# Window attention of a two-layer encoder: queries and keys projected with features on partitions, the rotary partner crossed by DMA, a third PSUM bank for scores

## The chip, the cores and the metric

The kernel runs on one core of a Trainium2 chip. A core has a matmul engine (TensorE, PE in the profile, with its weight load PEld), a vector engine (DVE), a scalar engine (ACT), a general engine (GpSimd, POOL), a queue engine (SyncE, SP) that issues transfers, and 16 DMA engines. Matmul results land in PSUM, which has 8 banks of 128 x 512 floats. The metric is device time in microseconds (us) of one execution.

## The reference

The program is an encoder of two layers over 1024 tokens of width 1024. Layer 0 mixes tokens by windowed attention and by cross-attention into 256 memory tokens, layer 1 by a gated recurrence; each ends in a convolutional feed-forward. The change touches the windowed attention alone: 16 query heads of 64 features, 4 key/value heads, rotary positions on queries and keys, each token looking 128 tokens to either side, and one sink per head.

```python
def rope(x, pos):
    ...
    x1, x2 = xf[..., :half], xf[..., half:]
    return jnp.concatenate([x1 * cos - x2 * sin, x2 * cos + x1 * sin], axis=-1).astype(x.dtype)

def mixer_window_attn(u, mem_kv, w_in, sink, w_out, pos):
    q, k, v, xq = jnp.split(u @ w_in, [ATT_Q_W, ATT_Q_W + ATT_KV_W, ATT_Q_W + 2 * ATT_KV_W], axis=-1)
    q = rope(q.reshape(bsz, t, ATT_HEADS, ATT_HEAD_DIM), pos)
    k = rope(k.reshape(bsz, t, ATT_KV_HEADS, ATT_HEAD_DIM), pos)
    ...
    o = window_gqa_sink(q, k, v, sink).reshape(bsz, t, ATT_Q_W)
    return jnp.concatenate([o, memory_cross_attn(xq, mem_kv)], axis=-1) @ w_out
```

## The kernel before

Float32 precision is kept by splitting each operand into a high and a low part and adding three matmuls (`mm3`, L79 to L82). The input of layer 0 stands transposed in `uh` and `ul`, features on partitions and tokens along the row. Its norm factor per token, `rs0`, is not in there: it is multiplied into the rotary tables (for queries and keys) and into v afterwards (`rooted`, L1375).

`window()` works through four groups, one per key/value head with its four query heads. `proj(g)` loads four weight units of 128x768 (`wunit`: load on SP, high part on ACT, low part on DVE or, by `QKV_POOL`, on POOL). For each of 8 tiles of 128 tokens, `token(t)` makes 24 matmuls with the tile of `uh` held still and 384 weight columns moving (256 for queries, 64 keys, 64 values), so a result has tokens on partitions. DVE multiplies it by the cosines (L285) and, with the two halves of each head swapped by an access pattern, by the sines (L286); POOL adds the two (L287, L288); ACT and DVE take v out (L290, L298). `turn(b, rqs)` then transposes four tiles at a time on TensorE into the bank `ptq` (L310), since scores need features on partitions, and ACT and DVE split the result out of PSUM: keys by `split`, queries into tiles that hold the high part on one half of the partitions and the low part on the other (L318 to L321).

`attend` makes the scores of one block of 128 queries and one head against up to 384 keys in a bank `ps` (L362, L363); DVE adds the mask, takes the maxima and moves them to `sm` (L365), ACT takes the exponentials (L372), ACT and DVE divide (L381, L383), TensorE transposes the probabilities into `pt` (L388), ACT and DVE split them into `ph` and `pl` (L85, L86), and TensorE multiplies them with v into `po` (L391, L392). Cross-attention units stand between. PSUM is dealt out as two banks `pj` for projections, one `ptq`, two `ps`, two `pt` and one `po`: all eight.

The code is written as attend(g), then proj(g+1); a tile scheduler with a timeline model of its own mixes the two when the program is built, and fixes each engine's order of instructions. On the chip each engine runs its list in order and waits at semaphores. On POOL's queue hang transfers for the feed-forward (`second_sums`, L143), one step of them behind each rotary addition (`sum_steps[0].send(done)`).

Of the kernel before, what the change touches and what calls it, by code (L numbers as in the profile page):

```python
# [31 lines left out]
QKV_POOL = (0, 2, 2, 2)  # L32
# [14 lines left out]
def build(tc, A, out):  # L47
# [36 lines left out]
    def split(h, l, src):  # L84
        act.copy(h, src)  # L85
        dve.tensor_tensor(l, src, h.bitcast(F32), op=ALU.subtract)  # L86
# [155 lines left out]
    def window():  # L242
# [10 lines left out]
        c4 = lambda ap: ap.rearrange("p (h a c) -> p h a c", a=2, c=32)  # L253

        tags = {"pj": ("pj", 2, psq), "ps": ("ps", 2, psp), "pt": ("pt", 2, psp), "po": [lambda: psp.tile([P, 512], F32, tag="po", bufs=1, name="po")] * 2, "sm": 3}
        xhead = [None]
        def pair(kind, i):
# [3 lines left out]
        units = [(h, b) for h in range(4) for b in range(2)]  # L261

        def proj(g):
            us = [wunit(A["wqkv"][g, u], 768, eng=pool if u < QKV_POOL[g] else None) for u in range(4)]
# [5 lines left out]
            def token(t):  # L270
                ps = psq.tile([P, 384], F32, tag="pj", bufs=2, name="pj")
                for k in range(KT):
                    wh, wl = us[k // 2]
                    c = slice((k % 2) * 384, (k % 2 + 1) * 384)
                    m = slice(t * P, (t + 1) * P)
                    mm3(ps, uh[:, k, m], ul[:, k, m], wh[:, c], wl[:, c], k == 0, k == KT - 1)
                if g == 0:
                    with tc.issue_after(roped[0].ins) if t else nullcontext():
                        rooted(t, cos[:, t], sin[:, t].rearrange("p a b -> p (a b)"))
                t1 = ea.tile([P, 320], F32, tag="t1", bufs=1, name="t1")  # L280
                t2 = ea.tile([P, 320], F32, tag="t2", bufs=1, name="t2")
                rq = ea.tile([P, 384], F32, tag="rq", bufs=5, name="rq")
                cb = bc(cos[:, t, :].unsqueeze(1).unsqueeze(1), [P, 5, 2, 32])
                sb = bc(sin[:, t, :, :].unsqueeze(1), [P, 5, 2, 32])
                dve.tensor_tensor(c4(t1), c4(ps[:, :320]), cb, op=ALU.mult)  # L285
                roped[0] = dve.tensor_tensor(c4(t2), c4(ps[:, :320])[:, :, ::-1, :], sb, op=ALU.mult)  # L286
                pool.tensor_tensor(rq[:, :320], t1, t2, op=ALU.add)  # L287
                done = pool.tensor_tensor(rq[:, 320:], t1[:, 256:], t2[:, 256:], op=ALU.add)  # L288
                sum_steps[0].send(done)
                cast = act.activation(v[:, t, :64], ps[:, 320:], AF.Copy, scale=rs0[:, t:t + 1])  # L290
                if g == 0 and t + 5 < NT:
                    tag = ("kh", "kl", "v")[t]
                    row = ap_.tile([P, NT, P] if tag == "v" else [P, T], F32R, tag=tag, bufs=1, name="row").bitcast(F32)
                    row = row.rearrange("p a b -> p (a b)") if tag == "v" else row
                    nc.sync.dma_start(row, A["x"][(t + 5) * P:(t + 6) * P, :])
                    with tc.issue_after(cast.ins):
                        act.activation(row, row, AF.Square, accum_out=xss[:, t + 5:t + 6])
                dve.scalar_tensor_tensor(v[:, t, 64:], ps[:, 320:], rs0[:, t:t + 1], v[:, t, :64].bitcast(F32),  # L298
                                         op0=ALU.mult, op1=ALU.subtract)
                return rq  # L300

            def turn(b, rqs):
                hs = slice(b * 512, (b + 1) * 512)
                for w in range(3) if (g, b) not in ((0, 0), (3, 1)) else (2, 0, 1):
                    if g or b or w == 2:
                        tp = psq.tile([P, 4, P], F32, tag="ptq", bufs=1, name="ptq")
                    else:
                        tp = psp.tile([P, 4, P], F32, tag="pt", bufs=2, name="ptq")
                    for tt in range(4):
                        pe.transpose(tp[:, tt, :], rqs[tt][:, w * P:(w + 1) * P], ident)  # L310
                    tp = tp.rearrange("p a b -> p (a b)")
                    if w == 2:
                        split(kh[:, hs], kl[:, hs], tp)
                    else:
                        lo, hi = slice(0, 64), slice(64, 128)
                        q0, q1 = [ap_.tile([P, 512], F32R, tag="qs", bufs=8, name="qs") for _ in range(2)]
                        qs[2 * w][b], qs[2 * w + 1][b] = q0, q1
                        act.copy(q0[lo], tp[lo])  # L318
                        dve.tensor_tensor(q0[hi], tp[lo], q0[lo].bitcast(F32), op=ALU.subtract)
                        act.copy(q1[hi], tp[hi])  # L320
                        dve.tensor_tensor(q1[lo], tp[hi], q1[hi].bitcast(F32), op=ALU.subtract)  # L321

            kept = (qs, kh, kl, v)
            if g == 0:
                rqs = [token(t) for t in range(5)]
                turn(0, rqs[:4])
                attend(0, kept, range(3))
                turn(1, rqs[4:] + [token(t) for t in range(5, NT)])
            else:
                for b in range(2):  # L330
                    turn(b, [token(t) for t in range(4 * b, 4 * b + 4)])
            return kept

        pairs, roped = {}, {}
# [9 lines left out]
        def attend(g, qkv, blocks=range(NT)):  # L344
            qs, kh, kl, v = qkv
            for b in range(2):
                for nn in range(4):
# [11 lines left out]
                    for j in range(4):  # L359
                        s = psp.tile([P, 384], F32, tag="ps", bufs=2, name="ps")  # L360
# [66 lines left out]
        wo0.begin(psq, ("pj", "pj", "ptq"), [y0[:, t, :] for t in range(NT)], {6: marks[3, 2], 7: marks[3, 2]})  # L427
# [944 lines left out]
    cos = tables.tile([P, NT, 32], F32, name="cos")  # L1372
    sin = tables.tile([P, NT, 2, 32], F32, name="sin")

    def rooted(t, *turns):  # L1375
        c = slice(t, t + 1)
        dve.tensor_scalar(xss[:, c], xss[:, c], 1.0 / D, EPS, op0=ALU.mult, op1=ALU.add)
        pool.tensor_tensor(rs0[:, c], xss[:, c], nhalf[:, c], op=ALU.pow)
        for x in turns:
            dve.tensor_scalar_mul(x, x, rs0[:, c])  # L1380
# [110 lines left out]
def prepare(i):  # L1491
# [23 lines left out]
    for g in range(4):  # L1515
        w = np.concatenate([aw[:, 256 * g:256 * g + 256], aw[:, 1024 + 64 * g:1024 + 64 * g + 64],
                            aw[:, 1280 + 64 * g:1280 + 64 * g + 64]], axis=1)
        qkv.append(w.reshape(4, 2, P, 384).transpose(0, 2, 1, 3).reshape(4, P, 768))
# [32 lines left out]
    a["cos"] = c(co.reshape(NT, P, 32).transpose(1, 0, 2))  # L1551
    a["sin"] = c(np.stack([-si, si], 1).reshape(NT, P, 2, 32).transpose(1, 0, 2, 3))
# [20 lines left out]
```

## Time and profile before

| | |
|---|---|
| time, median of 3 runs | 2656.88 us (2653.15 to 2657.52) |
| profiled execution, its own time | 2650.18 us |
| its span | 2648.4 us |
| TensorE busy | 98% of the span |
| the stage that the change touches | from about 55 us to about 430 us |

In a group's row of the profile the columns are line, engine, operation, output and input names, shape, count, busy time, mean ns of one, and then the idle time of the engine just before such instructions with what ended it. Matmuls are pipelined, so that a matmul's duration is longer than the time by which it moves the next one.

### The profile page before, as it was taken

To read this page: it belongs to the slowest core of one execution; us is meant where nothing else is said; L and a number is where in the kernel's file an instruction comes from. 1 tells how busy PE (TensorE), PEld (TensorE's weight loads), DVE (VectorE), ACT (ScalarE), POOL (GpSimd) and SP (SyncE) were. 2 spreads that over 40 slices of the span, in tenths; PEclk is the share of its full clock that TensorE was granted. 3 is DMA by queue.
4 is the path that set the end of the run, shared out by engine and by line. 5 is a ranking of instruction groups with operands and counts; after the bars stand their busy time and mean duration, and the time that the engine had idled before them with its cause. 6 is when DMAs were issued, how large, how long until landed. Compare 5 with 4: busy or idle time off the path is not lost. (4 is left out here: it accounts for less than half of the span.)

```text
span 2648.4 us, 38975 instructions
## 1 busy us (share of the span) xinstructions
PE 2595.5 (98%) x14372; PEld 2177.9 (82%) x14372; DVE 1768.2 (67%) x2948; ACT 1395.1 (53%) x2534; POOL 473.0 (18%) x520
## 2 busy tenths in 40 slices
PE   8999999999999999999999999999999999999998
PEld 7888887788888888887888888888887788888887
DVE  6788886578565655477668685876657665656447
ACT  6467676545444445455465564656434444444443
POOL 0321010211111100031224241322211111110013
PEclk9999999999999999999999999999999999999999
DMA  9782222367777756674235351113337778785666
GB/s 355 249 174 57 74 86 85 102 192 196 199 198 199 206 153 219 215 267 158 84 104 152 87 131 51 55 33 114 121 108 194 197 195 204 202 203 169 202 209 235
DMA packets 195727, 425.92 MB, mean 161 GB/s; under 512 B 20048, under 2 KB 56272, under 8 KB 189904
## 3 DMA queue, kind: packets, MB, share of 16 engines
q1 hardware_dynamic: 161552, 324.06, 37.9%
q0 software_dynamic: 24544, 90.19, 16.4%
q10 hardware_dynamic: 9440, 9.19, 1.0%
q8 instruction: 113, 1.85, 0.3%
q14 instruction: 78, 0.64, 0.1%
HBM read 330.04 MB, written 116.39 MB: 169 GB/s over the span
## 5 line engine op out<-in xcount | busy, mean ns | idle before, releaser
L86 DVE TENSOR_TENSOR wl<-st,wh 128x1024 fp32r<-128x1024 f32 (+1 forms) x238 | 262.4, 1109 | 316.6 <-ACT wh L85 286.1
L85 ACT CAST wh<-st 128x1024 fp32r<-128x1024 f32 (+1 forms) x238 | 222.2, 936 | 287.7 <-PE X L574 189.3
L80 PE MATMUL pj<-uh,wh 128*128 128x512 f32 x512 | 203.9, 399 | 2.8 <-DVE q L1129 1.3
L574 PE MATMUL X<-wh,wl 128*128 128x512 f32 x528 | 205.2, 390 | 0.0
L574 PE MATMUL X<-wl,wh 128*128 128x512 f32 x528 | 205.1, 390 | 0.0
L81 PE MATMUL pj<-ul,wh 128*128 128x512 f32 x512 | 202.6, 396 | 0.0
L82 PE MATMUL pj<-uh,wl 128*128 128x512 f32 x512 | 202.3, 395 | 0.0
L574 PE MATMUL X<-wh 128*128 128x512 f32 x528 | 198.9, 390 | 0.6 <-DVE c L1003 0.6
L80 PE MATMUL pj<-wh,uh 128*128 128x384 f32 (+1 forms) x512 | 189.1, 371 | 3.4 <-DVE xl L86 1.3
L82 PE MATMUL pj<-wh,ul 128*128 128x384 f32 (+1 forms) x512 | 187.2, 366 | 0.0
L81 PE MATMUL pj<-wl,uh 128*128 128x384 f32 (+1 forms) x512 | 187.1, 365 | 0.0
L574 PE MATMUL V<-uh,wh 128*128 128x512 f32 x336 | 130.9, 390 | 0.0
L574 PE MATMUL V<-ul,wh 128*128 128x512 f32 x336 | 130.9, 390 | 0.0
L574 PE MATMUL V<-uh,wl 128*128 128x512 f32 x336 | 130.9, 390 | 0.0
L76 DVE TENSOR_TENSOR wl<-st,wh 128x1024 fp32r<-128x1024 f32 (+1 forms) x91 | 112.1, 1236 | 24.7 <-ACT wh L75 22.7
L75 ACT CAST wh<-st 128x1024 fp32r<-128x1024 f32 (+1 forms) x97 | 97.7, 1014 | 39.5 <-PE pj L81 16.4
L574 PEld LDWEIGHTS X<-wh 128*128 128x128 f32 x528 | 99.2, 188 | 21.4 <-issue 1.0
L574 PEld LDWEIGHTS X<-wl,wh 128*128 128x128 f32 x528 | 99.2, 188 | 20.5
L574 PEld LDWEIGHTS X<-wh,wl 128*128 128x128 f32 x528 | 99.2, 188 | 20.5
L80 PEld LDWEIGHTS pj<-uh,wh 128*128 128x128 f32 x512 | 96.3, 188 | 22.0 <-DVE q L1129 1.8
L962 POOL TENSOR_TENSOR c<-c,g 128x512 f32<-128x512 f32 x24 | 43.8, 1843 | 389.3 <-PE X L574 319.4
L1225 POOL TENSOR_TENSOR E<-EP,q 128x256 f32<-128x256 f32 x64 | 61.4, 959 | 288.9 <-DVE EP L1218 272.7
(411 smaller groups left out, 7219.1 us busy)
## 6 DMA issues: line engine op xcount, KB each, us to landing
st<-hid SPq DMA_DIRECT2D x154, 256.0 KB, 3.2
st<-in_ffw_dram SPq DMA_DIRECT2D x108, 256.0 KB, 3.5
w2s<-in_ffw_dram POOLq DMA_DIRECT2D x24, 1024.0 KB, 8.4
st<-in_ffw_dram SPq DMA_DIRECT2D x46, 512.0 KB, 4.4
hid<-tt SPq DMA_DIRECT2D x88, 256.0 KB, 4.7
st<-w2s SPq DMA_DIRECT2D x88, 256.0 KB, 3.4
sx<-in_ffw_dram SPq DMA_DIRECT2D x84, 256.0 KB, 3.9
sy<-in_ffw_dram SPq DMA_DIRECT2D x42, 512.0 KB, 6.5
```

The costliest lines, as they stand in the source:

```text
L75: act.copy(h[:, :n], raw)
L76: (eng or dve).tensor_tensor(l[:, :n], raw, h[:, :n].bitcast(F32), op=ALU.subtract)
L80: pe.matmul(o, ah, bh, start=first, stop=False)
L81: pe.matmul(o, ah, bl, start=False, stop=False)
L82: return pe.matmul(o, al, bh, start=False, stop=last)
L85: act.copy(h, src)
L86: dve.tensor_tensor(l, src, h.bitcast(F32), op=ALU.subtract)
L574: last = pe.matmul(o, x, y, start=new, stop=e, skip_group_check=not first)
L962: pool.tensor_tensor(y[q][:, t, :], y[q][:, t, :], g3[:, c], op=ALU.mult)
L1225: pool.tensor_tensor(gl, pl_, ql, op=ALU.mult)
```

## The change

Features now stand on partitions from the start. A group's weights come as three units of 128x1024: one with 64 value and 64 key columns, two with 128 query columns (two heads) each. `project(u, b)` holds 128 weight columns still and moves 512 tokens, so one unit and one half of the tokens is 24 matmuls of 512 columns, and ACT copies the result to memory (`raw`, L304). The partner half of each head for the rotation is on other partitions, so DMAs on SP cross it over (`swapped`, L309). DVE multiplies the product by the cosines, POOL the crossed copy by the sines (L312), and POOL adds (L313); ACT and DVE split the sum, from memory in place of PSUM (L349 to L352, L85, L86). The 64 key rows are laid down twice, on both halves of the partitions, by DMA (L322). Values are transposed back to tokens on TensorE (L326). The tables become 128x1024 each and are scaled by a matmul of ones with the diagonal of the token factors (`scaled_tables`). The freed `ptq` bank becomes `ps2`, a third bank for scores, used for every third score tile.

```diff
-QKV_POOL = (0, 2, 2, 2)
+QKV_POOL = (0, 1, 1, 1)
...
+        def score():
+            scored[0] += 1
+            if scored[0] % 3:
+                return psp.tile([P, 384], F32, tag="ps", bufs=2, name="ps")
+            return psq.tile([P, 384], F32, tag="ps2", bufs=1, name="ps")
...
+        def temp(tag):
+            return ea.tile([P, 512], F32, tag=tag, bufs=2, name=tag)
+
+        def scaled_tables(b):
+            hs = slice(b * 512, (b + 1) * 512)
+            rooted(slice(4 * b, 4 * b + 4))
+            dg = temp("t1").rearrange("p (a b) -> p a b", a=4)
+            bank = psp.tile([P, 4, P], F32, tag="pt", bufs=2, name="pbc")
+            for t in range(4):
+                dve.tensor_scalar_mul(dg[:, t], ident, rs0[:, 4 * b + t:4 * b + t + 1])
+                pe.matmul(bank[:, t, :], ones, dg[:, t], start=True, stop=True)
+            bank = bank.rearrange("p a b -> p (a b)")
+            for x in (cos, sin):
+                dve.tensor_tensor(x[:, hs], x[:, hs], bank, op=ALU.mult)
...
+            def project(u, b):
+                hs = slice(b * 512, (b + 1) * 512)
+                wh, wl = us[u]
+                ps = psq.tile([P, 512], F32, tag="pj", bufs=2, name="pj")
                 for k in range(KT):
...
+                    c = slice(k * P, (k + 1) * P)
+                    mm3(ps, wh[:, c], wl[:, c], uh[:, k, hs], ul[:, k, hs], k == 0, k == KT - 1)
+                raw = temp("qa")
+                act.copy(raw, ps)
+                return ps, raw, hs
+
+            def swapped(o, lo, raw, at):
+                for a, z in ((0, 32), (32, 0)):
+                    nc.sync.dma_start(o[lo + a:lo + a + 32], raw[at + z:at + z + 32])
+
+            def rope(a, x, hs):
+                pool.tensor_tensor(x, x, sin[:, hs], op=ALU.mult)
+                done = pool.tensor_tensor(a, a, x, op=ALU.add)
+                for _ in range(2 if sent[0] % 3 == 0 else 1):
+                    sum_steps[0].send(done)
+                sent[0] += 1
+
+            def keys(b):
+                ps, raw, hs = project(0, b)
+                x, a = temp("qb"), temp("t1")
+                for lo in (0, 64):
+                    nc.sync.dma_start(a[lo:lo + 64], raw[64:])
+                    swapped(x, lo, raw, 64)
+                tp = psp.tile([P, 4, P], F32, tag="pt", bufs=2, name="ptv")
+                for t in range(4):
+                    pe.transpose(tp[:, t, :64], raw[:64, t * P:(t + 1) * P], ident[:64, :64])
+                if (g, b) == (0, 0):
+                    scaled_tables(0)
...
+                dve.tensor_tensor(a, a, cos[:, hs], op=ALU.mult)
+                rope(a, x, hs)
+                split(kh[:, hs], kl[:, hs], a)
+                return cast
+
+            def queries(w, b):
+                ps, raw, hs = project(1 + w, b)
+                x, a = temp("qb"), temp("t1")
+                for lo in (0, 64):
+                    swapped(x, lo, raw, lo)
+                dve.tensor_tensor(a, ps, cos[:, hs], op=ALU.mult)
+                rope(a, x, hs)
...
+                act.copy(q0[lo], a[lo])
+                dve.tensor_tensor(q0[hi], a[lo], q0[lo].bitcast(F32), op=ALU.subtract)
+                act.copy(q1[hi], a[hi])
+                dve.tensor_tensor(q1[lo], a[hi], q1[hi].bitcast(F32), op=ALU.subtract)
...
-                        s = psp.tile([P, 384], F32, tag="ps", bufs=2, name="ps")
+                        s = score()
...
-        wo0.begin(psq, ("pj", "pj", "ptq"), [y0[:, t, :] for t in range(NT)], {6: marks[3, 2], 7: marks[3, 2]})
+        wo0.begin(psq, ("pj", "pj", "ps2"), [y0[:, t, :] for t in range(NT)], {6: marks[3, 2], 7: marks[3, 2]})
```

Three places of the orders follow; the number behind a name tells apart the tiles of that name.

TensorE before, while group 1 is projected beside the attention of group 0: the tail of a token tile (`pj`), four transposes of its finished neighbours (`ptq` from `rq`), and attention behind them.

```order
L82 MATMUL pj_2015<-wh_1833,ul_78 128x384
L310 MATMUL ptq_1997<-ident_74,rq_1869 128x128 [waits DVE_49,PE_49]
L310 MATMUL ptq_1997<-ident_74,rq_1905 128x128
L310 MATMUL ptq_1997<-ident_74,rq_1941 128x128
L310 MATMUL ptq_1997<-ident_74,rq_1977 128x128
L391 MATMUL po_1311<-ph_1339,v_672 128x512 [waits Activation_49]
L362 MATMUL ps_1509<-kh_670,qs_1263 128x384 [waits DVE_49]
```

TensorE in the change, the end of the first long stretch without projection in the same part of the program: scores (`ps` from `kh`, `qs`), cross-attention (`po`), values turned back (`ptv`), and the next projection (`pj_2615`), which waits for DVE to have read the bank's last content.

```order
L399 MATMUL ps_2262<-kh_1757,qs_1856 128x384 [waits DVE_49]
L400 MATMUL ps_2262<-kl_1758,qs_1856 128x384
L80 MATMUL po_1711<-ph_1717,kvh_1552 128x512 [waits Activation_49]
L81 MATMUL po_1711<-pl_1718,kvh_1552 128x512
L82 MATMUL po_1711<-ph_1717,kvl_1553 128x512
L399 MATMUL ps_2266<-kh_1757,qs_1899 128x384 [waits DVE_49]
L400 MATMUL ps_2266<-kl_1758,qs_1899 128x384
L326 MATMUL ptv_1940<-ident_74,qa_1930 128x64 [waits PE_49]
L326 MATMUL ptv_1940<-ident_74,qa_1930 128x64 x3
L80 MATMUL pj_2615<-uh_77,wh_2609 128x512 [waits DVE_49]
```

The transposes of queries are gone, and the projection comes in larger pieces with longer stretches of attention between. Such stretches (no projection, over 2.5 us of TensorE work) stood before at two places in length: 28 transposes, 16 score matmuls of 384 columns, 12 of 256 and 16 of 512; and 26 of 384, 16 transposes and 4 of 512. In the change there are three: 32 transposes, 22 of 384, 12 of 256, 23 of 512 and 8 value transposes; 32, 22, 6, 24 and 8; 36, 22, 19, 28 and 8.

ACT before, around the query casts of group 1, first half (`qs` from the bank `ptq`).

```order
L318 CAST qs_2002<-ptq_1997 64x512 [waits PE_49]
L381 ACTIVATE sm_1421<-sm_1421,rd_1426 128x384 [waits DVE_49,Activation_49]
L381 ACTIVATE sm_1421<-sm_1421,rd_1426 128x384 [waits Activation_49]
L394 COPY o_1050<-po_1311 64x4x128 [waits PE_49]
L290 ACTIVATE v_1841<-pj_2015,rs0_86 128x64 [waits DVE_49]
L85 CAST ph_1402<-pt_1397 128x512 [waits PE_49,Activation_49]
L320 CAST qs_2003<-ptq_1997 64x512 [waits DVE_49]
```

ACT in the change, from a raw copy (`qa`) to the query casts of the same unit (`qs` from `t1`); L409 are the exponentials, L418 the divisions.

```order
L304 COPY qa_2934<-pj_2909 128x512 [waits DMAHW6_49,DMAHW5_49,DMAHW7_49,DMAHW0_49,PE_49]
L85 CAST ph_2244<-pt_2239 128x512 [waits PE_49]
L85 CAST ph_2293<-pt_2288 128x512 [waits DVE_49,PE_49]
L409 ACTIVATE sm_2397,su_2401<-sm_2397,nm_2399 128x384 [waits DVE_49]
L409 ACTIVATE sm_2397,su_2401<-sm_2397,nm_2399 128x384 x3
L407 ACTIVATE es_2400<-es_2400 128x4 [waits DVE_49]
L418 ACTIVATE sm_2397<-sm_2397,rd_2402 128x384 [waits DVE_49,Activation_49]
L418 ACTIVATE sm_2397<-sm_2397,rd_2402 128x384 [waits Activation_49]
L349 CAST qs_2945<-t1_2937 64x512 [waits Pool_49]
L351 CAST qs_2946<-t1_2937 64x512
```

A cast that waited for TensorE's transposes now waits for POOL's addition, and a copy stands ahead of it.

DVE in the change, in the first group, where the tables are scaled (`pbc` is the spread token factor). Before, each token tile had two small operations here on 128x32 and 128x64 of the tables.

```order
L286 TENSOR_TENSOR cos_92<-cos_92,pbc_714 128x512 [waits PE_49]
L286 TENSOR_TENSOR sin_93<-sin_93,pbc_714 128x512
L334 TENSOR_TENSOR t1_697<-t1_697,cos_92 128x512 [waits DMAHW3_49,DMAHW0_49,DVE_49]
L344 TENSOR_TENSOR t1_777<-pj_749,cos_92 128x512
L86 TENSOR_TENSOR kl_667<-t1_697,kh_666 128x512 [waits Activation_49]
L344 TENSOR_TENSOR t1_820<-pj_792,cos_92 128x512 [waits DVE_49]
```

The projection of the second half on TensorE (`pj_1057`) takes the bank of `pj_749`, so it follows the fourth of these rows; between the spreading matmuls and it, four matmuls of `pj_792` are left on TensorE.

More of the change, by code (lines that the diff above doesn't have):

```diff
@@ L261, in window @@
         units = [(h, b) for h in range(4) for b in range(2)]
+        ones = tables.tile([P, P], F32, name="ones")
+        pool.memset(ones, 1.0)
+        def temp(tag):
[11 more added lines that the diff above has]
+                dve.tensor_tensor(x[:, hs], x[:, hs], bank, op=ALU.mult)
         def proj(g):
-            us = [wunit(A["wqkv"][g, u], 768, eng=pool if u < QKV_POOL[g] else None) for u in range(4)]
+            us = [wunit(A["wqkv"][g, u], eng=pool if u >= 3 - QKV_POOL[g] else None) for u in range(3)]
             qs = [[None] * 2 for _ in range(4)]
@@ L269, in proj @@
             v = kvp.tile([P, NT, P], F32R, tag="v", bufs=1, name="v")
-            def token(t):
-                ps = psq.tile([P, 384], F32, tag="pj", bufs=2, name="pj")
+            def project(u, b):
+                hs = slice(b * 512, (b + 1) * 512)
+                wh, wl = us[u]
+                ps = psq.tile([P, 512], F32, tag="pj", bufs=2, name="pj")
                 for k in range(KT):
[L273 to L321, printed above, removed]
@@ new lines, in proj @@
+            kept = (qs, kh, kl, v)
+            for b in range(2):
+                cast = keys(b)
+                if g == 0 and b == 0:
+                    for t, tag in zip(range(5, NT), ("kh", "kl", "v")):
+                        row = ap_.tile([P, NT, P] if tag == "v" else [P, T], F32R, tag=tag, bufs=1, name="row").bitcast(F32)
+                        row = row.rearrange("p a b -> p (a b)") if tag == "v" else row
+                        nc.sync.dma_start(row, A["x"][t * P:(t + 1) * P, :])
+                        with tc.issue_after(cast.ins):
+                            act.activation(row, row, AF.Square, accum_out=xss[:, t:t + 1])
+                for w in range(2):
+                    queries(w, b)
+                if g == 0 and b == 0:
+                    scaled_tables(1)
+                    attend(0, kept, range(3))
@@ L1371, in build, with rooted @@
     tables = tc.alloc_tile_pool(name="tables", bufs=1, reuse_waits="tile")
[L1372 to L1376, printed above, removed]
+    cos = tables.tile([P, T], F32, name="cos")
+    sin = tables.tile([P, T], F32, name="sin")
+    def rooted(c):
         dve.tensor_scalar(xss[:, c], xss[:, c], 1.0 / D, EPS, op0=ALU.mult, op1=ALU.add)
         pool.tensor_tensor(rs0[:, c], xss[:, c], nhalf[:, c], op=ALU.pow)
-        for x in turns:
-            dve.tensor_scalar_mul(x, x, rs0[:, c])
         dve.tensor_scalar_mul(xsc[:, 0, c], rs0[:, c], XSCALE)
@@ L1550, in prepare @@
     co, si = np.cos(ang).astype(np.float32), np.sin(ang).astype(np.float32)
-    a["cos"] = c(co.reshape(NT, P, 32).transpose(1, 0, 2))
-    a["sin"] = c(np.stack([-si, si], 1).reshape(NT, P, 2, 32).transpose(1, 0, 2, 3))
+    a["cos"] = c(np.tile(co.T, (4, 1)))
+    a["sin"] = c(np.tile(np.concatenate([-si.T, si.T]), (2, 1)))
     q, j = np.arange(P)[:, None], np.arange(384)[None, :]
```

26 lines of the change are left out of this document (13 added, 13 removed).

## The prediction

> **What bounds the kernel now.** I read the page's busy times first, then windows around the edited stage, then the list of TensorE's waits in it, then single instructions. The profiled execution took 2650.18 us (its span 2648.4), 6.7 us less than the 2656.88 us median of the three runs shown, which lie between 2653.15 and 2657.52. Terms are worked out against the profiled execution and their sum is then set on the median.
>
> ```profile
> PE 2595.5 (98%) x14372; PEld 2177.9 (82%) x14372; DVE 1768.2 (67%) x2948; ACT 1395.1 (53%) x2534; POOL 473.0 (18%) x520
> 0.00:55.00 55.00, 47.45 (x293) 42.86 (x294) 37.21 (x52) 37.29 (x50) 1.70 (x8) 1.00 0.99 370
> 55.00:430.00 375.00, 353.45 (x2001) 313.19 (x2000) 292.60 (x788) 252.31 (x629) 71.84 (x101) 1.00 0.47 130
> 280.00:297.30 17.30, 17.30 (x94) 14.64 (x93) 13.40 (x34) 10.32 (x24) 0.00 (x0) 1.00 0.23 71
> 297.30:313.10 15.80, 13.49 (x74) 9.69 (x72) 13.45 (x44) 13.41 (x36) 0.00 (x0) 1.00 0.10 34
> 403.90:416.10 12.20, 9.86 (x48) 6.46 (x47) 11.66 (x35) 9.58 (x22) 0.00 (x0) 1.00 0.01 4
> ```
>
> The window rows give length, then busy time (and instructions) of PE, PEld, DVE, ACT and POOL, then granted clock, DMA share and GB/s. TensorE is the bound over the whole program. The edited stage is the second row, at a granted clock of 1.00. In it TensorE is full wherever projection matmuls stand between the attention's (280 to 297.3), and short of work where attention runs alone (297.3 and 403.9): there DVE is busy 85% and 96% of the time. So an edit pays if it takes matmul time away, and costs where it leaves attention without projections beside it.
>
> **The change part by part.** First the matmuls, from starts of neighbours in the timeline (start, duration):
>
> ```profile
> 313.85 0.40 PE L80 MATMUL pj<-uh,wh 128*128 128x512 f32 x1
> 318.42 0.40 PE L82 MATMUL pj<-uh,wl 128*128 128x512 f32 x1
> 318.65 0.28 PE L80 MATMUL ps<-kvh,xh 128*128 128x256 f32 x1
> 319.25 0.28 PE L82 MATMUL ps<-kvh,xl 128*128 128x256 f32 x1
> 320.07 0.60 PE L388 MATMUL pt<-ident,sm 128*128 128x128 f32 x4
> 320.42 0.48 PE L392 MATMUL po<-pl,v 128*128 128x512 f32 x1
> 324.32 0.34 PE L80 MATMUL pj<-wh,uh 128*128 128x384 f32 x1
> 327.12 0.33 PE L81 MATMUL pj<-wl,uh 128*128 128x384 f32 x1
> L80 PE MATMUL pj<-wh,uh 128*128 128x384 f32 x256 | 87.4, 343 | 2.2 <-DVE xl L86 1.3 <-DVE v L298 1.0
> L310 PE MATMUL ptq<-ident,rq 128*128 128x128 f32 x96 | 17.7, 276 | 2.3 <-POOL rq L288 1.1 <-POOL rq L287 0.9 <-DVE qs L321 0.3
> ```
>
> Durations overlap in the pipeline, so what counts is the step. Between the first two rows lie 20 steps of 512 columns: 4.57/20 = 0.2285 us. 256 columns: 0.60/5 = 0.12. Four transposes: 0.35, so 0.0875 each. 384 columns: 2.80/16 = 0.175.
> - Projections: 3 x 256 = 768 matmuls of 384 columns become 576 of 512 (4 groups x 3 units x 2 halves x 24): 576 x 0.2285 - 768 x 0.175 = **-2.8**.
> - The 96 transposes of queries and keys go: 96 x 0.0875 = **-8.4**. Their waits go too (last row: 1.1 + 0.9 + 0.3): **-2.3**.
> - 32 transposes of v (128x64) come. No row has this shape; between nothing and a full transpose, 0 to 2.8. I take the nearest row: **+2.8**. The 8 matmuls that spread the token scale: 8 x 0.0875 = **+0.7**.
>
> The sure part is thus -10.0 us on the engine that is full. What stands against it is waiting:
>
> ```profile
> PE ps L362 <- DVE mx L365: 7.9, 13, 1.5
> L365 DVE CUSTOM_DVE_ANT_0 sm<-ps,wmask,sk 128x384 f32<-128x384 f32 x84 | 50.1, 612 | 17.0 <-PE ps L363 14.7 <-PE pt L388 2.0
> ```
>
> - Third score bank. TensorE waits 7.9 us, in 13 places, for DVE to empty one of two score banks. A third lets it run one tile of 612 ns ahead. Waits under that length vanish, the longest (1.5) only shrink, and where DVE is full nothing is gained: between -7.9 and 0, I take **-5**.
> - Attention alone. Read from the instruction orders, stretches with over 2.5 us of attention and no projection hold 65.5 us of TensorE work before and 84.0 after, by the steps above; the long ones are the two windows before, and three stretches after (counts in the section on the change) of 14.0, 13.6 and 16.4. The window at 297.3 holds 28 transposes, 16 steps of 384, 12 of 256 and 16 of 512: 2.5 + 2.8 + 1.4 + 3.7 = 10.4 us of work in 15.8. The one at 403.9 holds 26 of 384, 16 transposes and 4 of 512: 6.9 in 12.2. Together 10.7 us are lost on 17.3, or 0.62 per us. DVE needs 13.45 + 11.66 = 25.1 us for the same, so even with no idle time in DVE 7.8 are lost, 0.45 per us. Moving 18.5 us more attention there costs 18.5 x 0.45 = 8.3 at that limit. The three long stretches at 0.62 would cost 44.0 x 0.62 = 27.3 against 10.7, +16.6. If what is lost belongs to the attention and not to its place, nothing. Bounds 0 and +16.6; I take **+8**, the DVE limit, which is the row nearest to it.
>
> Then the longer chain of each unit:
>
> ```profile
> L85 ACT CAST kh<-ptq 128x512 fp32r<-128x512 f32 x8 | 4.7, 588 | 0.6 <-PE ptq L310 0.5
> L86 DVE TENSOR_TENSOR kl<-ptq,kh 128x512 fp32r<-128x512 f32 x8 | 5.5, 682 | 0.9 <-ACT kh L85 0.9
> L287 POOL TENSOR_TENSOR rq<-t,t 128x320 f32<-128x320 f32 x32 | 29.9, 934 | 270.8 <-DVE t L286 140.4 <-PE pt L388 27.7 <-DVE xss L1377 26.1
> oT<-o SPq DMA_DIRECT2D x24, 128.0 KB, 2.5
> L285 DVE TENSOR_TENSOR t<-pj,cos 128x320 f32<-128x320 f32 x32 | 15.5, 485 | 5.7 <-PE pj L82 5.5
> L372 ACT ACTIVATE sm<-sm,nm 128x384 f32<-128x384 f32 x84 | 50.7, 607 | 9.8 <-DVE nm L368 9.7
> L372 ACT ACTIVATION_READ_ACCUMULATOR sm<-sm,nm 128x1 f32 x112 | 21.1, 189 | 0.0
> 196.76 1.23 SPq L406 DMA_DIRECT2D oT<-o  x2
> ```
>
> - From the end of a unit's matmuls to the query casts: copy 0.59, crossing 2.5 (128 KB, the nearest row), two POOL operations of 128x512, each 0.934 x 512/320 = 1.5: 6.1. The crossing is four issues; two took 1.23 (last row), so the fourth may leave 1.8 later: 7.9. ACT reaches the casts in order, and behind them stand the probability casts that TensorE's L428 waits for. In the tight place shown in the section on the change ACT has between copy and cast two casts, four exponentials with their sums, two scalings and a small one: 2 x 0.59 + 4 x 0.80 + 2 x 0.61 + 0.2 = 5.8. So ACT waits 0.3 to 2.1 us there; the order has some 8 such places, 2.4 to 17 us of ACT. TensorE sees between none of it and all; I take **+2**, the short crossing, as the row is for one issue.
> - DVE and ACT themselves: DVE loses 64 rope operations (64 x 0.485 = 31.0) and gains 24 of 0.68 (16.3), 4 on the tables (2.7), and 1.2 on wider weight splits, ACT gains 24 copies (14.1). Both have room beside projections (77% and 60% in 280 to 297.3), so **0**; where that cover is gone is the term above. The swaps put 112 issues on SP ahead of weight loads that are issued a unit (24 x 0.2285 = 5.5 us) early; that and the second-sum sends on POOL, 32 as before, **0**, with any lateness inside the 17 above.
> - Scaling the tables: the first bank of the second half's projection is free only after four DVE operations behind the spreading matmuls, 4 x 0.68 = 2.7, less four matmuls still queued on TensorE, 0.9: **+1.8** (0 if the keys' DMA is late anyway, 3.6 if both halves pay).
> - Start: tables of 1 MB in place of 384 KB are 640 KB more in a stretch whose DMA engines are full (0.99, 370 GB/s): 0.64/0.37 = **+1.7**, or nothing if the tables' place in the queue has slack.
>
> Sum: -2.8 - 8.4 - 2.3 + 2.8 + 0.7 - 5 + 8 + 2 + 1.8 + 1.7 = -1.5. That is 2648.7 us for the profiled execution, and **2655.4** on the median.
>
> [...]
>
> ```profile
> 391.11 2.28 POOL L287 TENSOR_TENSOR rq<-t,t 128x320 f32<-128x320 f32 x1 [1.87 <-DVE t L286]
> 394.83 0.88 POOL L287 TENSOR_TENSOR rq<-t,t 128x320 f32<-128x320 f32 x1 [1.16 <-DVE t L286]
> 391.47 1.20 DVE L76 TENSOR_TENSOR wl<-st,wh 128x1024 fp32r<-128x1024 f32 x1
> ```
>
> The same addition took 2.28 us with a DVE operation on two memory operands beside it and 0.88 without. After the change the 32 query splits and 8 key splits read two memory operands where they read PSUM before, the 8 key products too, and POOL has 48 wide operations. [...]
>
> **Rivals.**
> - **Room is found** (faster). The third bank removes all 7.9 (2.9 more), and the attention's losses don't depend on its place (8 less): 2655.4 - 10.9 = **2644.5**. For it: most of the 13 waits are short, and the total of attention is unchanged. Against it: DVE at 96% in the last window.
> - **DVE takes the stretches** (slower). With DVE full in the three long stretches the third bank gives nothing, since TensorE then waits for DVE whatever the number of banks (+5: that edit does not do what it says), and each stretch loses 0.62 per us (16.6 in place of 8): 2655.4 + 13.6 = **2669**. It decides where DVE's busy share in a stretch passes 90%. For it: 85% and 96% in the two windows of before. Against: the change takes some 11 us from DVE overall.
> [...]
>
> **How the numbers follow.** A measurement can tell about 0.2% (5.3 us) from no change. Chances: the forecast 0.34 (own range 2649 to 2662; split 0.07 faster, 0.24 the same, 0.03 slower), room is found 0.32 (0.28 faster, 0.04 the same), DVE takes the stretches 0.24 (0.03 the same, 0.21 slower), shared port 0.10 (half the same, half slower). That makes 0.35 faster, 0.36 the same, 0.29 slower. All low bounds together give 2656.9 - 20.7 = 2636, all high ones 2656.9 + 28.9 = 2686; neither end needs fewer than four terms at their limits at once, so the range of 2640 to 2671 takes in every case, with 2 to 4 us around the outer ones.
>
> **What would show it.** Right: TensorE's instructions by group fall by the 8.4 and 2.8; its waits for the score maxima (L402) fall below 3 us; windows over the three stretches show DVE over 90% busy and TensorE losing 0.4 to 0.6 per us; ACT's query casts (L349, L351) wait for POOL 1 to 2 us in a few places. [...]

## The result, and the profile after

The changed kernel takes 2696.24 us (median of 4 runs, 2693.46 to 2698.06), the kernel before 2656.89: 1.015 of it, with a 95% interval of 1.0133 to 1.0168. It is 39 us slower, outside the range of the prediction, and above the 2686 us that all its high bounds together gave. The two profiled executions, from which the rows below come, lie 46.5 us apart (2696.72 and 2650.18).

The page of the changed kernel, busy times:

```profile
PE 2614.1 (97%) x14132; PEld 2159.8 (80%) x14132; DVE 1768.2 (66%) x2885; ACT 1409.6 (52%) x2554; POOL 487.3 (18%) x496
```

TensorE has 240 instructions fewer and is busy longer. Windows tell where. First the kernel before, the edited stage and the rest:

```profile
55.00:520.00 465.00, 440.91 (x2419) 384.87 (x2418) 346.29 (x896) 301.26 (x736) 85.91 (x109) 1.00 0.44 123
520.00:2640.00 2120.00, 2105.86 (x11659) 1749.39 (x11658) 1381.60 (x1994) 1055.86 (x1747) 384.87 (x402) 1.00 0.57 164
```

The same for the changed kernel, the rest from 40 us later on:

```profile
55.00:520.00 465.00, 416.15 (x2002) 333.47 (x2002) 324.95 (x813) 298.19 (x722) 91.47 (x77) 0.96 0.48 131
560.00:2680.00 2120.00, 2106.43 (x11655) 1748.51 (x11654) 1380.41 (x1990) 1055.59 (x1745) 383.11 (x404) 1.00 0.57 164
```

The last 2120 us are the same in everything. Nearly all is lost ahead of them, in the stage, where TensorE's granted clock fell to 0.96. The stage is bounded by its first projection and the first feed-forward matmul (`X`). Before:

```profile
54.86 0.33 PE L80 MATMUL pj<-wh,uh 128*128 128x384 f32 x1
572.76 0.48 PE L574 MATMUL X<-uh,xwh 128*128 128x512 f32 x1
```

After:

```profile
60.56 0.40 PE L80 MATMUL pj<-uh,wh 128*128 128x512 f32 x1
617.80 0.48 PE L611 MATMUL X<-uh,xwh 128*128 128x512 f32 x1
```

It starts 5.7 us later and lasts 557.2 in place of 517.9 us, 39.3 more. By the steps of single matmuls, TensorE's work in it is 7.0 us less (2.8 and 8.4 less; 2.8 and 1.4 more for 32 value transposes and 16 spreading matmuls). Its waits between 55 and 520 us add up to 48.1 in place of 23.1 us, 25 more. The clock of 0.96 over 465 us is some 19 us, of which about 3 fall into the waits themselves. That places 34 of the 39.3 us; the other 5 are not placed. The largest waits of TensorE after (total, times, longest):

```profile
PE po L428 <- ACT ph L85: 9.8, 3, 5.0
PE po L428 <- DVE o L432: 7.0, 7, 1.7
PE pj L80 <- DVE t L344: 6.1, 5, 3.3
PE ps L399 <- DVE mx L402: 5.4, 7, 1.1
PE pt L232 <- DVE pl L86: 5.2, 4, 2.5
PE pt L425 <- DVE v L332: 5.0, 1, 5.0
```

Before, none was over 1.5 us. After, four are over 3 us: 3.3 at 161, 5.0 at 175, 4.5 at 262 and 5.0 at 456. The first two can be followed through the timeline (start, duration, in brackets the idle time ahead and its releaser). TensorE:

```profile
157.46 0.27 PE L400 MATMUL ps<-kl,qs 128*128 128x256 f32 x1
161.06 0.80 PE L80 MATMUL pj<-uh,wh 128*128 128x512 f32 x1 [3.33 <-DVE t L344]
...
169.50 0.60 PE L425 MATMUL pt<-ident,sm 128*128 128x128 f32 x4
175.12 0.80 PE L428 MATMUL po<-ph,v 128*128 128x512 f32 x1 [5.02 <-ACT ph L85]
```

ACT, POOL and SyncE over the same time:

```profile
159.70 0.58 ACT L304 COPY qa<-pj 128x512 f32<-128x512 f32 x1 [5.76 <-DMA qb<-qa]
172.19 0.62 ACT L349 CAST qs<-t 64x512 fp32r<-64x512 f32 x1 [5.28 <-POOL t L313]
```

```profile
169.56 1.26 POOL L312 TENSOR_TENSOR qb<-qb,sin 128x512 f32<-128x512 f32 x1 [5.46 <-DMA qb<-qa]
170.90 1.26 POOL L313 TENSOR_TENSOR t<-t,qb 128x512 f32<-128x512 f32 x1
```

```profile
160.35 3.07 SPq L309 DMA_DIRECT2D qb<-qa  x4
```

At 161 a raw copy had stood 5.76 us for a buffer that an earlier unit's crossing was still reading; DVE's product and the projection bank stood behind it. That crossing was issued from 145.44 on, while second-sum transfers of up to 1 MB filled the DMA engines (a DMA share of 1.05 from 145 to 155), and landed at about 159.7. At 175, four crossings were issued from 160.35 to 163.42, POOL got their data at 169.56, ACT its sum at 172.19, and the probability cast that TensorE needed stood behind that cast in ACT's order: 11.9 us from the end of the raw copy to the query cast, where the prediction counted 5.5 to 7.3 (its 6.1 to 7.9 less the copy). The median of the 96 crossing transfers in the stage is 2.5 us, as the prediction had it; the longest landing is 13.6 us, in the crossing issued from 145.44 on:

```profile
qb<-qa SPq DMA_DIRECT2D x96, 64.0 KB, 2.5
```

And the clock, in windows over the first of these, another place, the wait at 175 and one of 1.74 us at 344.5 (clock third from the right):

```profile
157.50:161.00 3.50, 0.23 (x3) 0.03 (x1) 0.68 (x3) 1.27 (x3) 1.23 (x1) 0.97 0.19 63
161.00:164.00 3.00, 2.94 (x7) 2.36 (x8) 2.90 (x7) 1.92 (x4) 2.92 (x4) 0.50 0.49 93
164.50:167.50 3.00, 3.00 (x15) 2.47 (x14) 1.18 (x4) 2.41 (x9) 0.00 (x0) 1.00 0.91 177
109.50:112.70 3.20, 3.20 (x12) 2.72 (x10) 3.20 (x12) 1.88 (x6) 0.16 (x1) 0.52 1.02 401
174.50:181.50 7.00, 6.38 (x20) 5.50 (x21) 4.94 (x16) 4.65 (x14) 0.00 (x0) 0.51 1.02 202
345.00:348.50 3.50, 2.81 (x11) 2.33 (x11) 1.91 (x5) 1.85 (x5) 0.00 (x0) 0.52 0.03 5
```

At 161, behind 3.3 us without work, the granted clock was 0.50 for 3 us (second row): 7 matmuls started in place of some 13 at 0.2285 us a step. In windows of half a microsecond the fall cost 1.7 us, half as much again as that wait, and the one behind the wait of 5.0 us at 175 cost 3.4 us (7 us at 0.51). The fourth row is a fall to 0.52 where the recorded waits ahead were 0.40 and 0.95 us, around eight transposes, with no other matmul from 106.7 to 109.6. Windows of half a microsecond over the stage show eight such falls, 18.8 us in all: 11.9 behind the four waits over 3 us, 6.9 behind shorter ones (the longest ahead of each 0.95, 1.74, 1.34 and 2.52 us).

### The profile page after: what moved, and what is told of

Same layout as the page of the kernel before. It is cut to its first block, busy times and chain, and to the rows that moved or that the text cites. A ratio compares the mean times of both kernels' runs of the same rounds, so it can differ in the third digit from the quotient of the medians.

```text
span 2694.6 us, 38562 instructions
## 1 busy us (share of the span) xinstructions
PE 2614.1 (97%) x14132; PEld 2159.8 (80%) x14132; DVE 1768.2 (66%) x2885; ACT 1409.6 (52%) x2554; POOL 487.3 (18%) x496
## 5 line engine op out<-in xcount | busy, mean ns | idle before, releaser
L86 DVE TENSOR_TENSOR wl<-st,wh 128x1024 fp32r<-128x1024 f32 (+1 forms) x238 | 262.3, 1109 | 317.1 <-ACT wh L85 282.5
L85 ACT CAST wh<-st 128x1024 fp32r<-128x1024 f32 (+1 forms) x238 | 222.4, 936 | 293.9 <-PE X L611 195.6
L80 PE MATMUL pj<-uh,wh 128*128 128x512 f32 x704 | 282.8, 402 | 8.0 <-DVE t L344 6.1
L81 PE MATMUL pj<-ul,wh 128*128 128x512 f32 x704 | 279.8, 397 | 0.0
L82 PE MATMUL pj<-uh,wl 128*128 128x512 f32 x704 | 278.6, 396 | 0.0
L82 PEld LDWEIGHTS pj<-uh,wl 128*128 128x128 f32 x704 | 133.8, 190 | 27.2
L81 PEld LDWEIGHTS pj<-ul,wh 128*128 128x128 f32 x704 | 134.2, 191 | 25.8 <-DVE ul L86 0.4
L76 DVE TENSOR_TENSOR wl<-st,wh 128x1024 fp32r<-128x1024 f32 x90 | 115.9, 1289 | 31.3 <-ACT wh L75 29.5
L75 ACT CAST wh<-st 128x1024 fp32r<-128x1024 f32 x93 | 97.1, 1048 | 45.1 <-PE pj L81 33.0
L80 PE MATMUL pj<-wh,uh 128*128 128x512 f32 x256 | 101.6, 397 | 1.2 <-DVE gs L1152 1.2
```

The costliest lines, as they stand in the source:

```text
L75: act.copy(h[:, :n], raw)
L76: (eng or dve).tensor_tensor(l[:, :n], raw, h[:, :n].bitcast(F32), op=ALU.subtract)
L80: pe.matmul(o, ah, bh, start=first, stop=False)
L81: pe.matmul(o, ah, bl, start=False, stop=False)
L82: return pe.matmul(o, al, bh, start=False, stop=last)
```

## The experiments

Each is an edit of the changed kernel (2696 us); "stage" is the time from the first projection to the first `X`, 557.2 in the change and 517.9 before. The scheduler mixes each kernel anew when it is built, so every time below is that of an edit together with the order that it brought. The orders differ much: of the 2415 instructions of TensorE in the stage of g1_cos_anchored, the longest common sequence (by operation and tiles) holds 2266 in h2_pool_beside, 2144 in h8_dma_between, 2066 in h3_cross_beside and 1958 in the change. What an order is worth by itself no run shows.

**Late second sums.**

```diff
-                for _ in range(2 if sent[0] % 3 == 0 else 1):
+                for _ in range(9 if sent[0] >= 22 else 0):
```

> The change, with the 18 steps of second-sum transfers sent behind the last two rotary additions instead of one or two behind each of the first 14. Everything else as in the change (2696 us). Theory A, the crossing comes late because its small DMAs share the 16 DMA engines with the second-sum transfers: the gaps of 3.3 and 5.0 us at 161 and 175 us and that at 262 vanish with the slow clock behind them, 2672 to 2684 us. Theory B, the crossing is late by its own four issues and landing, traffic or none: 2690 to 2697. Theory C, DVE is full in the stretches without projections and the crossing is no matter: 2693 to 2698.

Measured: 2714.84 us. The gaps at 161, 175 and 262 went, but TensorE's waits from 55 to 520 us were 43.7 us (48.1 in the change), and the late transfers held up the loads of the output projection:

```profile
522.73 0.80 PE L80 MATMUL pb<-wh,oh 128*128 128x512 f32 x1 [10.05 <-ACT oh L85]
540.75 0.80 PE L80 MATMUL pb<-wh,oh 128*128 128x512 f32 x1 [9.28 <-ACT oh L85]
```

So the traffic makes single gaps, but most of the waits up to 520 us stay without it. Theory A falls as the whole cause.

**Scores in two banks.**

```diff
-            if scored[0] % 3:
+            if True:
                 return psp.tile([P, 384], F32, tag="ps", bufs=2, name="ps")
```

> The change with all scores in the two banks of before, the third left empty. If the third bank gave the 5 us that the prediction took for it: 2699 to 2703 us. If it gives nothing, because DVE empties the tiles at the same rate: 2693 to 2698. If the scheduler's other order matters more than the bank: anything from 2680 to 2710.

Measured: 2692.23 us (2691.80 to 2692.66). Four us faster without the third score bank, in another order: no gain of it shows.

**The partner crossed by POOL.**

```diff
-                    nc.sync.dma_start(o[lo + a:lo + a + 32], raw[at + z:at + z + 32])
+                    zs = slice(at + z, at + z + 32)
+                    pool.tensor_tensor(o[lo + a:lo + a + 32], raw[zs], sin[zs, hs], op=ALU.mult)
...
-                pool.tensor_tensor(x, x, sin[:, hs], op=ALU.mult)
-                done = pool.tensor_tensor(a, a, x, op=ALU.add)
+                done = pool.tensor_tensor(a, a, x, op=ALU.subtract)
```

(and the keys' two copies made by DVE from PSUM)

> The change without DMAs for the partner: POOL multiplies the raw copy by the sines in four pieces of 32 partitions and writes each to its partner's partitions, then subtracts; DVE takes the two copies of the keys straight from PSUM. POOL's part becomes 5 x 1.3 = 6.5 us long, but it waits for no transfer, and the raw copy's buffer is free when POOL has read it. Theories A and B (the crossing by DMA is the cost): 2655 to 2670 us, granted clock above 0.995. Theory C: 2685 to 2698, no better than the change.

Measured: 2701.27 us, clock 0.991. It is above every theory's range, C's 2685 to 2698 being the nearest. The chain here is five POOL operations long, so the run does not clear the chain.

**No crossing.**

```diff
-                pool.tensor_tensor(x, x, sin[:, hs], op=ALU.mult)
+                pool.tensor_tensor(x, raw, sin[:, hs], op=ALU.mult)
```

(and the DMAs taken out, the keys' two copies made by DVE from PSUM)

> The change without crossing at all: the sines are multiplied with the raw copy itself, so queries and keys get no partner in their rotation (the computation that is left out), and the two copies of the keys come from PSUM by DVE. Shows what the rest of the change is worth. Theories A and B: 2645 to 2658 us, as the sure part of the sum is -10 us against before. Theory C: 2680 to 2696.

Measured: 2678.76 us, stage 543.0. It takes 17 us off; 24 stay. That is just below theory C's range and far above that of A and B.

**A bank for the value transposes; four raw buffers.**

```diff
-                tp = psp.tile([P, 4, P], F32, tag="pt", bufs=2, name="ptv")
+                tp = psq.tile([P, 4, P], F32, tag="ps2", bufs=1, name="ptv")
```

> The change with the bank ps2 given to the value transposes in place of every third score tile, so that they no longer take their turn in the two pt banks behind all of the former group's probabilities. Theory D: a value transpose that waits for the end of that attention holds one of the two raw buffers; the other query copies go through a single buffer, or stop, their projection banks stay full and attention is left alone. By D the first long stretch (197 to 218 us in the change) goes, the waits of copies for the crossing DMAs shrink, idle time of TensorE between 55 and 520 us falls from 48 to 30 to 38 us, and the time from 2692 (two score banks alone) to 2668 to 2682. Theory B (the crossing's own lateness): 2688 to 2697, since the crossing is as it was.

```diff
-STAGE = 4
+STAGE = 3
...
-            return ea.tile([P, 512], F32, tag=tag, bufs=2, name=tag)
+            return ea.tile([P, 512], F32, tag=tag, bufs=4 if tag == "qa" else 2, name=tag)
```

> The change with four raw buffers in place of two, paid for by three weight staging tiles in place of four; the value transposes stay in the pt banks. Theory D: held raw buffers no longer stop the copies, so the first long stretch goes as in the former run: 2665 to 2685 us, less if one staging tile fewer costs nothing. Theory B: 2688 to 2700.

Measured: 2698.26 and 2722.55 us. In the first the long stretch near 200 us did go, and with it none of the time: TensorE's waits were 46.4 us, in other places, and against the run with two score banks alone (2692.23) it lost 6 us. The second also has a staging tile fewer, whose cost was not run alone, so it says little. Theory D's range fits neither.

**Late tables.** Both table loads moved behind the last `part(KT - 1)`.

> The change with the two rotary tables loaded behind the last part of the transposed input, in place of ahead of most of it. In the change the first projection starts at 60.6 us, before at 54.9. If the tables' extra 640 KB are the cause: first projection at 55 to 57 us and 2690 to 2693 us in all. If they are not: 60 to 61 and 2695 to 2698.

Measured: 2696.49 us. Its first projection:

```profile
56.82 0.39 PE L80 MATMUL pj<-uh,wh 128*128 128x512 f32 x1
```

So 3.7 of the 5.7 us at the start are the tables; but hardly any of it arrived at the end, where `X` began at 617.0 (617.8 in the change).

**The partner crossed by ACT.**

```diff
-                    nc.sync.dma_start(o[lo + a:lo + a + 32], raw[at + z:at + z + 32])
+                    act.copy(o[lo + a:lo + a + 32], raw[at + z:at + z + 32])
```

(with `ps` passed for `raw`, the raw copy kept for the value rows, and the keys' two copies made by DVE from PSUM)

> The change with the partner crossed by ACT in place of DMA: four copies of 32 partitions from the projection bank, each to its partner's partitions; the raw copy is made for value rows alone, and DVE takes both copies of the keys from PSUM. No query unit needs a raw buffer any more, so by theory D the first long stretch goes here too, and the chain has no DMA. ACT has some 24 x 3 x 0.58 = 42 us more to do. D and B together: 2655 to 2675 us. If ACT becomes the bound: 2685 to 2700. Theory B alone would give about what the run without crossing gave, 2679, or a little more.

Measured: 2698.30 us. ACT was busy 343 of 465 us, 45 more than in the change; that ACT's copies took what the DMA's absence gave is likely, not shown.

**Cosines alone; no rotation.** In the first, `rope` and the crossing go; in the second queries and keys are split from the bank.

```diff
-                dve.tensor_tensor(a, ps, cos[:, hs], op=ALU.mult)
-                rope(a, x, hs)
+                done = dve.tensor_tensor(a, ps, cos[:, hs], op=ALU.mult)
+                rope(done)
```

> The change with queries and keys multiplied by the cosines alone: crossing, the multiplication by the sines and POOL's addition are left out; the raw copy, the banks and everything else stay. The run without crossing still lost 24 us against before. Theory P, what is left there is that ACT's and DVE's query splits queue behind POOL's two operations of 1.3 us: 2650 to 2662 us. Theory G, it is the coarse projection itself (units of 24 matmuls of 512 in two banks that DVE and ACT free late) and the order that follows from it: 2670 to 2682, little better than 2679.

> The change with no rotation at all: queries and keys are split by ACT and DVE straight out of the projection bank, as before out of the transposes; the raw copy is made for values alone. DVE has 40 us less to do than before and TensorE 7 us less. Left out: crossing, both tables' products, POOL's operations. Theory P: 2640 to 2655. Theory G: 2665 to 2685, since the units are as coarse and banks wait for room in the query tiles. If under 2650, projection with features on partitions is worth what was counted for it and all of the loss is in the rotation's chain.

Measured: 2759.80 and 2758.85 us. Both are spoiled by a side effect: with no POOL operation to follow, the second-sum transfers all went at the start, and TensorE stood some 45 us for weights, 14 and 25 us at once in the first:

```profile
88.31 1.22 PE L80 MATMUL pb<-wh,mh 128*128 128x512 f32 x2 [14.27 <-ACT wh L75]
118.90 0.58 PE L80 MATMUL pb<-mh,wh 128*128 128x256 f32 x1 [25.26 <-ACT wh L75]
```

Their stages alone were short, 529.0 and 528.4 us, but had no such transfers in them.

**A third projection bank.**

```diff
-"pj": ("pj", 2, psq)
+"pj": ("pj", 3, psq)
...
-        wo0.begin(psq, ("pj", "pj", "ps2"),
+        wo0.begin(psq, ("pj", "pj", "pj"),
```

(scores in two banks)

> The whole change with the freed bank as a third projection bank and scores in two. Theory G (projection stops because its two banks are freed late): 2665 to 2680. Theory B, crossing and order: 2688 to 2700.

Measured: 2683.02 us, stage 544.0: 13 us off the change, 9 off the two-bank run. Between the two theories' numbers.

**Cosines alone, with POOL's place kept.**

```diff
-                pool.tensor_tensor(x, x, sin[:, hs], op=ALU.mult)
-                done = pool.tensor_tensor(a, a, x, op=ALU.add)
+                done = pool.tensor_tensor(mark, done, done, op=ALU.add)
```

(and no DMA for the keys, whose two copies DVE makes from PSUM)

> As f1_cos_only (cosines alone; crossing, sines and POOL's addition left out), but a POOL operation on one column stands where POOL's addition stood, so that the second-sum transfers go when they go in the change. In f1_cos_only they all went at the start, which cost some 70 us of waiting for weights there; from its first projection to the first feed-forward matmul it took 529 us against 557 in the change and 518 before. If the rotation's chain behind the projection (crossing, then two POOL operations) is 28 of the 39 us lost in the stage: 2665 to 2672 us. If f1's stage was short only because no second sums were running beside it: 2678 to 2690.

Measured: 2664.11 us (2661.91 to 2665.01), the kernel before beside it 2653.41; ratio 1.0035, 1.0022 to 1.0049. Its stage window and the longest waits of TensorE in it:

```profile
55.00:520.00 465.00, 435.69 (x2164) 351.47 (x2163) 327.97 (x841) 310.50 (x744) 32.88 (x54) 1.00 0.42 121
```

```profile
PE pj L80 <- DVE t L340: 6.2, 7, 2.7
PE ps L395 <- DVE mx L398: 3.9, 6, 1.2
```

The clock is back at 1.00, the waits add up to 29.1 us, and the stage is 521.2. So 32 of the 39 us hang on the chain of crossing, sines and addition, with the order that goes with it. What is left, 13.1 us between the profiled executions, is a start 5.4 us later (first projection at 60.27), 3.3 us in the stage and 4.4 behind it. The long stretches of attention alone are all there:

```profile
179.70:201.20 21.50, 18.09 (x94) 12.55 (x92) 17.89 (x59) 17.52 (x48) 2.37 (x1) 1.00 0.23 65
271.30:294.80 23.50, 20.45 (x113) 14.92 (x111) 21.07 (x63) 18.65 (x50) 0.00 (x0) 1.00 0.21 57
392.30:412.10 19.80, 15.88 (x76) 11.47 (x74) 17.87 (x52) 14.44 (x39) 0.00 (x0) 0.91 0.43 125
```

**Deferred splits.** Each unit's splits are kept in a list and issued behind the next raw copy.

```diff
-                act.copy(raw, ps)
+                flush(act.copy(raw, ps))
...
+            def flush(after=None):
+                while pending:
+                    with tc.issue_after(after.ins) if after else nullcontext():
+                        pending.pop(0)()
```

> The whole change, with the splits of each unit's rotated sum put behind the raw copy of the next unit in ACT's order (some 5 us or more later), so that ACT and DVE, which go in order, do not stand before a sum that POOL has not finished. Theory Q (the chain costs what it costs because its last step stands in ACT's and DVE's queues): ACT's waits for POOL fall from 15.4 us to under 4 and the time to 2672 to 2682. If the chain's cost is that queries themselves come late, or banks: 2690 to 2700.

Measured: 2692.45 us. ACT's waits in it:

```profile
ACT qs L355 <- POOL t L318: 11.0, 6, 3.8
ACT qa L304 <- DMA qb<-qa: 9.4, 2, 5.5
```

In the change they were:

```profile
ACT qs L349 <- POOL t L313: 15.4, 6, 5.3
ACT qa L304 <- DMA qb<-qa: 10.0, 2, 5.8
```

One unit's delay was too little to clear them, so theory Q was hardly tested.

**Third projection bank with cosines alone, and with deferred splits and late tables.** Edits as above, together.

> As g1_cos_anchored, with the freed bank as a third projection bank and scores in two. If chain and projection banks are the two parts of the loss and add up, 28 and 13 us: 2652 to 2660 us, level with before. If they are one and the same loss seen twice: as g1_cos_anchored, 2663 to 2672.

> The whole change with deferred splits, the freed bank as a third projection bank, scores in two, and the tables loaded late. If theory Q and the banks both hold and add up: 2658 to 2672 us. If only the banks: 2680 to 2686.

Measured: 2660.87 us (2658.00 to 2663.21) and 2681.50. With the full chain the third projection bank gives 13 us, without it 3: mostly one and the same loss seen twice. It looks as if the bank covers part of the time for which the chain holds results. No version with the full rotation came near the kernel before.

**One property of the chain at a time,** added to the cosine kernel: POOL's work with nobody waiting for it (two operations of 128x512 a unit, on the tables); the crossing with nobody reading it; a plain DMA between product and splits.

```diff
+                pool.tensor_tensor(x, cos[:, hs], sin[:, hs], op=ALU.mult)
+                done = pool.tensor_tensor(x, x, cos[:, hs], op=ALU.add)
```

> [...] Theory R, the chain's length is what costs: 2662 to 2668 us. [...]

```diff
+                    swapped(x, lo, raw, lo)
```

> As g1_cos_anchored, with the four crossing DMAs of each unit issued into a buffer that nobody reads: their traffic, SyncE's issuing and their hold on the two raw buffers are there, the wait of the sum for them is not. Theory R (the sum's wait): 2662 to 2668 us. Theory T (the raw copies stand for the buffers that the crossing holds, and behind them ACT and the projection banks): 2672 to 2684.

```diff
+                z = temp("qb")
+                nc.sync.dma_start(z, a)
+                a = z
```

> As g1_cos_anchored, with one DMA of 256 KB between the product and the splits: the chain is longer by some 3 us, with no POOL and one issue in place of four. Theory R (length alone): 2674 to 2684 us, a good half of the 32 us by which the change is behind g1. If length costs nothing by itself: 2662 to 2668.

Measured: 2705.77, 2677.14 and 2693.06 us against 2664.11, so +42, +13 and +29. The third lengthens the chain without POOL and without the crossing (one issue of 256 KB a unit, median landing 2.8 us, longest 16.0), and with its order gives nearly the change's whole loss. In its list, ACT waits for that DMA:

```profile
ACT qs L351 <- DMA qb<-t: 23.5, 6, 8.9
...
ACT kh L85 <- DMA qb<-t: 13.3, 4, 5.4
```

36.8 us of ACT's time, up to 8.9 at once. The first shows an effect of its own. DVE, then POOL:

```profile
173.22 11.37 DVE L349 TENSOR_TENSOR qs<-t,qs 64x512 fp32r<-64x512 f32 x1
184.62 0.17 DVE L404 TENSOR_SCALAR nm<-mx 128x4 f32<-128x4 f32 x1
```

```profile
173.92 2.80 POOL L316 TENSOR_TENSOR qb<-qb,cos 128x512 f32<-128x512 f32 x2
...
181.34 2.69 POOL L315 TENSOR_TENSOR qb<-cos,sin 128x512 f32<-128x512 f32 x2
```

A query split of 0.69 us took 11.37, and ended 0.56 us behind POOL's run of operations back to back (181.34 + 2.69 = 184.03). POOL had got behind, since second-sum transfers on its queue wait for one another (11.2 us in six places), and worked off its backlog in one go. This one hold can explain some 11 of the 42 us; the rest is open. In the change POOL's operations come in pairs and average 1.35 us, and no query split took over 1.5 us. But DVE's scalings (L383, then L420, and L227) took 42.4 us there, 38.5 before, and 31.9 in g1, where POOL does little (32.88 in place of 91.47 us busy from 55 to 520). Against g1 that is 10.5 us more in the change and 6.6 before; that POOL's work is the cause is not shown, nor what of it reached TensorE, and h8 loses its 29 us with scalings of 32.7 us and no such POOL work. The three don't add up to 32; whether that is the chain or the orders, they can't tell.

## Why the prediction was wrong

- **The projection's own sums were nearly right.** 240 instructions fewer, 7.0 us less work against a predicted 7.7 (the trace has 16 spreading matmuls where 8 were counted), the rest of the program unchanged.
- **The longer chain, taken at +2, is where it failed.** Leaving the chain out takes 32 us off, near twice the high bound of 17. Three things in that step were wrong. The crossing's landing was taken at a median, 2.5 us, which the trace bears out; but one at 160 us came some 6 us behind its last issue, and the longest took 13.6. ACT's wait was counted at the query cast alone (15.4 us in the trace, within the 2.4 to 17 of the prediction), but raw copies also waited 10.0 us for buffers that the crossing holds. And TensorE was taken to see little of ACT's waiting, while its own waits grew by 25 us. h8_dma_between, with a chain longer by one DMA in place of all that, loses 29 us. The room that the prediction found in ACT (60% busy in 280 to 297.3) is a mean, which says nothing about an engine that goes in order and stands.
- **There was no term for the clock.** The prediction read 1.00 in the stage before and went on from there. The slower clock, 0.96 from 55 to 520 us, cost some 16 to 19 us, the 3 between them falling into the waits. Of 18.8 us, 11.9 came behind waits of 3.3 to 5.0 us, where before none was over 1.5, and 6.9 behind shorter ones.
- **Attention alone, taken at +8 with bounds 0 and 16.6.** The three stretches came where the order had them:

```profile
196.90:217.70 20.80, 18.17 (x98) 12.95 (x97) 18.08 (x58) 17.53 (x48) 2.38 (x1) 1.00 0.51 137
299.80:321.30 21.50, 17.85 (x93) 12.54 (x91) 19.33 (x60) 17.54 (x48) 0.00 (x0) 1.00 0.22 65
417.00:442.80 25.80, 21.29 (x115) 16.43 (x114) 21.57 (x60) 18.53 (x46) 0.00 (x0) 0.93 0.42 114
```

  68.1 us for 44.0 of work, 24.1 lost, 0.55 per us, inside the predicted 0.45 to 0.62 and 13 more than before. The size was fair, but these stretches don't explain the 39 us: e10_ptv_bank lost the first of them and no time, and g1_cos_anchored has three of 64.8 us together and a stage only 3.3 us longer than before, with 7.0 us less work. That leaves 10 us at most for them there, near the 8 taken.
- **Third score bank, taken at -5.** TensorE's waits for the maxima fell from 8.9 to 5.4 us in that window, not below 3 as forecast, and without the bank the kernel is 4 us faster, in another order.
- **DVE's own work, taken at some 11 us less,** is 1768.2 us on both pages; 3.9 us of the difference are the longer scalings; the rest stays open.
- **Tables.** The scaling's wait of 1.8 was 1.65, at 80 us; the start, taken at +1.7, was 5.7, of which the tables' place explains 3.7 and the end shows none.
- **The rivals.** "DVE takes the stretches" had the right side with the wrong mechanism: DVE was busy 87%, 90% and 84% there. That DVE and POOL share a port, as the name "shared port" in the chances has it, no run shows; POOL's 128x512 operations averaged 1.35 us, and DVE's scalings took 3.9 us more than before. No rival had the chain as its mechanism, and none reached 2696.

What stays open: why the chain of before, which also went through POOL, cost so little. It ended in transposes on TensorE fed from five `rq` tiles, while that of the change ends in ACT's and DVE's own queues with two buffers at each step; that this is the reason is argued, not shown, as the one run with more raw buffers had a staging tile fewer. Open too is how much of the 32 us is the waiting itself and how much the order that the scheduler made of a longer chain: no run held the order fixed.

## What to carry to other kernels

When a step moves into another chain, price the chain by its slowest landing and by every buffer it holds, and look at what stands behind its last step on each engine that goes in order; a busy share of 60% is no cover there. Where TensorE has long waits that it did not have before, read the granted clock in short windows behind them: here a fall cost 1.7 us behind a wait of 3.3 and 3.4 us behind one of 5.0, half to two thirds as much again, and four falls stood behind waits of no more than 0.95 to 2.52 us. And if several repairs each move the waits without shortening the time, leave the suspect out altogether and put its properties back one by one.

## What the hardware showed

The clock fell to 0.52 without any recorded wait over 0.95 us, around eight transposes (109.5 to 112.7 us). In h2_pool_beside a DVE operation on two memory operands took 11.37 us, up to 0.56 us past the end of eight POOL operations in a row (173.92 to 184.03), where one such POOL operation took some 1.4 (2.80 for two) and another DVE split of the same shape, at 184.82, took 0.69. By what it was held so long is not shown.
